# Two score tiles lengthened by 32 bytes, so that the tiles behind them start at multiples of 128 bytes

## The chip, the cores and the metric

The kernel runs on one core of one Trainium2 chip. The metric is device microseconds of one execution; a comparison is made between medians of several executions on the same chip. Before the change the median of three runs is 1702.7 us (1699.94 to 1705.26).

## What is computed

Two layers of a diffusion trunk over 256 latent tokens (x) and 256 context tokens (ctx), width 1024, in 32-bit floats. Cut to what matters:

```python
for i in range(2):
    x   = x   + 0.5 * gt1 * swiglu(modulate(x,   g1, sh1, sc1), ffn1_wi[i], ffn1_wo[i])
    ctx = ctx + 0.5 * cg1 * swiglu(modulate(ctx, g1, ch1, cs1), ffn1_wi[i], ffn1_wo[i])
    hx, hc = modulate(x, g2, sh2, sc2), modulate(ctx, g2, ch2, cs2)
    if i == 0:   # convolution module, width 31, latent and context apart
        y_lat, y_ctx = conformer_conv(hx, ...), conformer_conv(hc, ...)
    else:        # 16 query heads, 4 key heads, window 128, sink, all context keys
        y_lat, y_ctx = windowed_gqa_sink(hx, hc, ...)
    x = x + gt2 * y_lat
    x = x + 0.5 * gt3 * swiglu(modulate(x, g3, sh3, sc3), ffn2_wi[i], ffn2_wo[i])
    if i == 0:   # the context is dropped after layer 1's mixer
        ctx = ctx + cg2 * y_ctx
        ctx = ctx + 0.5 * cg3 * swiglu(modulate(ctx, ...), ffn2_wi[i], ffn2_wo[i])
return rmsnorm(x, final_g)

def swiglu(h, w_in, w_out):          # w_in 1024 x 5632, w_out 2816 x 1024
    gate, up = jnp.split(h @ w_in, 2, axis=-1)
    return (silu(gate) * up) @ w_out
```

## The kernel before, in words

**Products.** Each 32-bit number is split into a high part (hi, rounded to the matmul's fp32r format) and the rest (lo). A product is three matmuls: hi weights with high values, hi weights with low values, lo weights with high values (`mm3`, lines 222, 223 and 224). The helper is `mm3(o, wh, wl, xh, xl, first, last)`: the weights are the stationary operand (128x128, loaded before each matmul), the values are the moving operand that is streamed through, with 512 columns where latent and context tokens go together and 256 where one of them goes alone.

**Tiles.** Normalised values lie in HH (high) and HL (low), eight slices of 512 columns, 2048 bytes of a partition each. The middle values of an FFN lie in MH and ML in the same way; the same memory holds QH and QL of attention. Blocks of weights (1 MB) come by DMA into `raw`, ScalarE writes `hi`, VectorE or GpSimd writes `lo`, four buffers of each. The FFN (`ffn`) takes a block for each of 22 slices of the middle (`g` and `u` accumulate the gate and the up product, `glu_end` writes `sg`, `mt` and then MH and ML) and 12 blocks for the way out (`o`). Layer 1's first FFN and its last have the same code; the last runs on the latent tokens alone (256 columns).

**Where other operands are streamed.** In attention, `qkv_mm` makes the values the stationary operand for k in (4, 5): there a `hi` or `lo` weight tile is the moving one (`o<-hi,HH`). In the convolution `taps_t` streams slices of UH and UL: for channel group 4 one contiguous piece of 256 columns per tap, whose start goes 4 bytes further with every tap (`uh[:, k:k + T]`): tap 16 starts 16 bytes over a multiple of 128, tap 17 starts 20 over, tap 28 starts 64 over. The normalisation streams `dg` (line 280).

**Memory.** The program places tiles once, pool behind pool in the order in which they are opened (const, rawp, hip, lop, adap, work, small, hp, mp). A pool holds, for each tag, its number of buffers times the longest tile that is ever asked of the tag. So one longer tile in a tag moves everything behind it, in the whole program. `mt` is a tag of the pool work with two buffers: in the FFNs a tile of 512 numbers (2048 bytes), in attention a score tile of 528 (2112 bytes), of which 513 are used (`homes`, line 1074).

The addresses that the built program gives, in bytes of a partition, and what is left over a multiple of 128:

| tile | before | over | after | over |
|---|---|---|---|---|
| hi (4), lo (4) | 67200 and on, 99968 and on | 0 | the same | 0 |
| mt (2) | 145216, 147328 | 64, 0 | 145216, 147360 | 64, 32 |
| sg (2) | 149440, 151488 | 64 | 149504, 151552 | 0 |
| t2, sq (2 each) | 153536 and on | 64 | 153600 and on | 0 |
| dg (2) | 157760, 158784 | 64 | 157824, 158848 | 0 |
| HH | 160448 | 64 | 160512 | 0 |
| HL | 176832 | 64 | 176896 | 0 |
| MH, QH | 193216 | 64 | 193280 | 0 |
| ML, QL | 209600 | 64 | 209664 | 0 |

Slices of HH, HL, MH and ML begin 1024 or 2048 bytes apart, so what is left over a multiple of 128 is that of the tile.

**Order.** In the FFNs a scheduler orders the work of each engine; in the start, the convolution and attention it is written out by hand (the strings SEQ, SEQ2 and SEQ3). Neither reads an address.

Of the kernel before, what the change touches and what calls it, by code (L numbers as in the profile page):

```python
# [11 lines left out]
F32 = mybir.dt.float32  # L12
# [5 lines left out]
P = 128  # L18
# [74 lines left out]
def trunk(ctx, tc, a, out):  # L93
# [6 lines left out]
    work = ctx.enter_context(tc.tile_pool(name="work", bufs=2))  # L100
# [969 lines left out]
    homes = []  # L1070
    for _ in range(3):
        z = adap.tile([P, 2, 520], F32, tag="adaw", name="S")
        homes.append([z[:, h, :513] for h in range(2)])
    homes.append([work.tile([P, 528], F32, tag="mt", name="S")[:, :513] for _ in range(2)])
    soft, PT, acc_wo = {}, {}, {}

    def scores(i):
# [232 lines left out]
def _build(nc, arrays):  # L1310
    aps = {k: nc.dram_tensor(f"in_{k}", v.shape, mybir.dt.from_np(v.dtype), kind="ExternalInput").ap()
           for k, v in arrays.items()}
    out = nc.dram_tensor("out_0", (P, CT, T), F32, kind="ExternalOutput").ap()
    with tile.TileContext(nc, schedule_with_timeline_sim=True) as tc:
        trunk(tc, aps, out)
# [12 lines left out]
```

## Time and profile before

| | |
|---|---|
| median of 3 runs | 1702.7 us (1699.94 to 1705.26) |
| profiled execution, its own time | 1699.08 us |
| its span, first to last instruction | 1697.3 us |
| mean granted TensorE clock | 0.98 |
| TensorE matmul busy | 97% of the span |
| VectorE, GpSimd, ScalarE busy | 66%, 48%, 36% |
| DMA | 252.14 MB, mean 149 GB/s |

A busy time of TensorE is the union of its matmuls, which overlap: a matmul's own duration is longer than the distance from its start to the next one's start. Where matmuls follow each other without a wait, that distance, the pitch, is what one more matmul costs. It is read from the timeline as the difference of two starts over the number of matmuls between them.

### The profile page before, as it was taken

Reading aid. Unit: us, or ns where it says so; the run is one execution under the profiler, and the core shown is the slowest. Engines: PE = TensorE matmul, PEld = TensorE weight load, DVE = VectorE, ACT = ScalarE, POOL = GpSimd, SP = SyncE. Lnnn points to the kernel's source line nnn. Section 1 sums busy time; section 2 is a strip of 40 time slices with the busy share of each in tenths; the row PEclk is TensorE's granted clock in tenths of the full one; section 3 lists DMA queues with packets and bytes.
Section 4 is the critical chain, followed back from the end, with each engine's and each line's share of the span. In section 5 each row is a group of like instructions: output and inputs, shape, how many; then the busy total and the mean of one; then the engine's idle time right before and its main releaser. Section 6 shows DMA issues by size and latency. Waiting matters only on the chain.

```text
span 1697.3 us, 23550 instructions
## 1 busy us (share of the span) xinstructions
PE 1644.3 (97%) x9333; PEld 1421.3 (84%) x9333; DVE 1114.0 (66%) x1717; ACT 612.4 (36%) x1015; POOL 811.0 (48%) x614
## 2 busy tenths in 40 slices
PE   9999999998898899999999999999999999999997
PEld 7788888888788888888888898888888888889997
DVE  4597789757799785745546376776545376567553
ACT  3522222234445663212222333222222245555443
POOL 2234324254867654556565546585565437410013
PEclk8999999999999899999999999999999989989999
DMA  7655455441213333433443324455554212246452
GB/s 280 235 181 198 167 186 213 159 149 52 98 63 136 137 114 111 186 138 117 150 154 138 111 75 149 175 193 203 175 196 155 100 50 76 90 169 237 164 193 69
DMA packets 48638, 252.14 MB, mean 149 GB/s; under 512 B 5264, under 2 KB 7312, under 8 KB 30992
## 3 DMA queue, kind: packets, MB, share of 16 engines
q1 hardware_dynamic: 48528, 250.64, 41.2%
q8 instruction: 73, 1.20, 0.3%
q14 instruction: 37, 0.30, 0.1%
HBM read 249.57 MB, written 1.05 MB: 148 GB/s over the span
## 4 chain that ended last, share of the span: by engine, by line
PE 85%; DVE 8%; issue 3%; ACT 2%; POOL 1%; DMA 1%; POOLq 0%; DVEq 0%; SPq 0%; ACTq 0%
PE o L222 9%; PE o L223 9%; PE o L224 9%; PE g L222 8%; PE u L222 8%; PE g L224 8%; PE g L223 8%; PE u L224 8%; PE u L223 8%; DVE A L725 3%; PE gu L544 2%; PE ug L222 1%; DVE HL L337 1%; PE ug L223 1%; PE ug L224 1%
## 5 line engine op out<-in xcount | busy, mean ns | idle before, releaser
L186 POOL TENSOR_TENSOR lo<-raw,hi 128x512 fp32r<-128x512 f32 (+1 forms) x388 | 602.9, 1585 | 683.3 <-ACT hi L183 543.6
L183 ACT ACTIVATE hi<-raw 128x1024 fp32r<-128x1024 f32 (+3 forms) x344 | 278.4, 866 | 575.6 <-PE u L223 256.2
L244 DVE CUSTOM_DVE_ANT_0 junk<-adaw,srow,par 128x1024 bf16<-128x1024 f32 x224 | 384.6, 1717 | 5.4 <-DMA adaw<-in_adaT 0.7
L222 PE MATMUL o<-MH,hi 128*128 128x512 f32 (+1 forms) x788 | 269.6, 344 | 0.0
L224 PE MATMUL o<-MH,lo 128*128 128x512 f32 (+1 forms) x788 | 268.1, 342 | 0.0
L223 PE MATMUL o<-ML,hi 128*128 128x512 f32 (+1 forms) x788 | 268.0, 342 | 0.0
L223 PE MATMUL g<-HL,hi 128*128 128x512 f32 (+1 forms) x712 | 251.8, 355 | 5.3 <-DVE HL L337 5.3
L222 PE MATMUL g<-HH,hi 128*128 128x512 f32 (+1 forms) x712 | 252.9, 357 | 2.8 <-ACT HH L333 2.8
L222 PE MATMUL u<-HH,hi 128*128 128x512 f32 (+1 forms) x712 | 252.9, 356 | 0.0
L224 PE MATMUL u<-HH,lo 128*128 128x512 f32 (+1 forms) x712 | 252.2, 354 | 0.0
L224 PE MATMUL g<-HH,lo 128*128 128x512 f32 (+1 forms) x712 | 252.2, 354 | 0.0
L223 PE MATMUL u<-HL,hi 128*128 128x512 f32 (+1 forms) x712 | 251.5, 353 | 0.0
L228 DVE TENSOR_TENSOR ML<-mt,MH 128x512 fp32r<-128x512 f32 (+1 forms) x92 | 106.2, 1154 | 129.0 <-ACT MH L227 128.9
L224 PEld LDWEIGHTS o<-MH,lo 128*128 128x128 f32 x788 | 147.8, 188 | 19.1
L223 PEld LDWEIGHTS o<-ML,hi 128*128 128x128 f32 x788 | 147.8, 188 | 18.2
L222 PEld LDWEIGHTS o<-MH,hi 128*128 128x128 f32 x788 | 147.6, 188 | 18.0 <-ACT MH L227 0.3
L354 DVE SCALAR_TENSOR_TENSOR X<-o,g,X 128x256 f32<-128x256 f32 x168 | 75.2, 479 | 126.5 <-PE o L224 126.4
L406 DVE TENSOR_TENSOR mt<-sg,u 128x512 f32<-128x512 f32 (+1 forms) x89 | 53.0, 595 | 159.4 <-PE u L224 141.7
L223 PEld LDWEIGHTS g<-HL,hi 128*128 128x128 f32 x712 | 134.0, 189 | 25.7 <-DVE HL L337 6.4
L222 PEld LDWEIGHTS g<-HH,hi 128*128 128x128 f32 x712 | 134.2, 189 | 22.5 <-ACT HH L333 3.9
L224 PEld LDWEIGHTS g<-HH,lo 128*128 128x128 f32 x712 | 134.4, 189 | 20.2
L224 PEld LDWEIGHTS u<-HH,lo 128*128 128x128 f32 x712 | 134.3, 189 | 20.3
(205 smaller groups left out, 2565.2 us busy)
## 6 DMA issues: line engine op xcount, KB each, us to landing
raw<-in_wi SPq DMA_DIRECT2D x85, 1024.0 KB, 4.9
adaw<-in_adaT SPq DMA_DIRECT2D x128, 512.0 KB, 3.7
raw<-in_wo SPq DMA_DIRECT2D x32, 896.0 KB, 4.8
raw<-in_wo SPq DMA_DIRECT2D x20, 1024.0 KB, 5.6
raw<-in_pw SPq DMA_DIRECT2D x12, 1024.0 KB, 4.8
raw<-in_dwd SPq DMA_DIRECT2D x8, 1024.0 KB, 4.9
ch<-in_ada SPq DMA_DIRECT2D x6, 1024.0 KB, 11.0
raw<-in_qkv SPq DMA_DIRECT2D x6, 1024.0 KB, 4.8
```

The costliest lines, as they stand in the source:

```text
L183: nc.scalar.activation(out=hi[:, q:q + w], in_=raw[:, q:q + w], func=AF.Copy)
L186: eng.tensor_tensor(out=lo[:, z:e], in0=raw[:, z:e], in1=hf[:, z:e], op=ALU.subtract)
L222: nc.tensor.matmul(o, wh, xh, start=first, stop=False)
L223: nc.tensor.matmul(o, wh, xl, start=False, stop=False)
L224: return nc.tensor.matmul(o, wl, xh, start=False, stop=last)
L228: return i_, nc.vector.tensor_tensor(out=lo, in0=src, in1=hif, op=ALU.subtract)
L244: nc.vector.tensor_tensor_reduce(out=junk, in0=wt, in1=srow[:, s, :], scale=1.0, scalar=pcol(O_ADAB, 72 * l + t), op0=ALU.mult, op1=ALU.ad ...
L337: return nc.vector.scalar_tensor_tensor(out=HL[:, c, SL[s]], in0=t2, scalar=sh, in1=HHf[:, c, SL[s]], op0=ALU.add, op1=ALU.subtract)
L354: return nc.vector.scalar_tensor_tensor(out=X[:, c, SL[s]], in0=psrc, scalar=gate, in1=X[:, c, SL[s]], op0=ALU.mult, op1=ALU.add)
L406: nc.vector.tensor_tensor(out=mt[:, :n], in0=sg[:, :n], in1=u[:, :n], op=ALU.mult)
L544: nc.tensor.matmul(gu[k][q], w[:, o:o + P], h[:, c, :], start=c == 0 and h is HH and w is hi, stop=c == 7 and w is lo)
L725: nc.vector.scalar_tensor_tensor(out=d, in0=src(k, z), scalar=wk(c, k), in1=d, op0=ALU.mult, op1=ALU.add)
```

## The change

The two score tiles of the tag `mt` get 536 numbers where they had 528, so each of the two buffers of the tag is 32 bytes longer. What is used of them stays 513 numbers. All that lies behind the first of the two moves: the second buffer by 32 bytes, everything behind it by 64. Each engine has the same instructions in the same order as before, and the DMA queues the same transfers.

```diff
@@ -1071,7 +1071,7 @@
     for _ in range(3):
         z = adap.tile([P, 2, 520], F32, tag="adaw", name="S")
         homes.append([z[:, h, :513] for h in range(2)])
-    homes.append([work.tile([P, 528], F32, tag="mt", name="S")[:, :513] for _ in range(2)])
+    homes.append([work.tile([P, 536], F32, tag="mt", name="S")[:, :513] for _ in range(2)])
     soft, PT, acc_wo = {}, {}, {}
```

## Rows read from the trace of the kernel before

**Rows 1.** The page: busy time of TensorE, and the chain that ended last by engine.
```profile
PE 1644.3 (97%) x9333; PEld 1421.3 (84%) x9333; DVE 1114.0 (66%) x1717; ACT 612.4 (36%) x1015; POOL 811.0 (48%) x614
...
PE 85%; DVE 8%; issue 3%; ACT 2%; POOL 1%; DMA 1%; POOLq 0%; DVEq 0%; SPq 0%; ACTq 0%
```

**Rows 2.** Busy time by stretch (an FFN; 1.5 us of attention): columns as its header says.
```profile
core 0: us, PE busy (x) PEld busy (x) DVE busy (x) ACT busy (x) POOL busy (x), PEclk, DMA share, GB/s
170.00:400.00 230.00, 230.00 (x1086) 192.16 (x1085) 171.89 (x230) 61.56 (x85) 83.61 (x53) 1.00 0.45 165
1373.00:1374.50 1.50, 1.50 (x9) 1.50 (x9) 1.09 (x3) 0.76 (x2) 0.00 (x0) 0.50 0.90 382
```

**Rows 3.** Timeline (start us, us, engine line op): TensorE at 1373, granted clock 0.50.
```profile
1373.20 0.41 PE L223 MATMUL o<-HL,hi 128*128 128x256 f32 x1
...
1374.27 0.41 PE L222 MATMUL o<-HH,hi 128*128 128x256 f32 x1
```

**Rows 4.** Timeline: TensorE in layer 0's first FFN, first and last of 28 matmuls.
```profile
199.79 0.39 PE L224 MATMUL u<-HH,lo 128*128 128x512 f32 x1
...
205.97 0.39 PE L224 MATMUL g<-HH,lo 128*128 128x512 f32 x1
```

**Rows 5.** Timeline: TensorE in the last FFN, first and last of 19 matmuls.
```profile
1599.77 0.28 PE L223 MATMUL u<-HL,hi 128*128 128x256 f32 x1
...
1601.89 0.28 PE L223 MATMUL g<-HL,hi 128*128 128x256 f32 x1
```

**Rows 6.** Groups by line and shape: matmuls whose moving operand is HH, HL, MH or ML.
```profile
L222 PE MATMUL u<-HH,hi 128*128 128x512 f32 x472 | 185.5, 393 | 0.0
...
L222 PE MATMUL o<-MH,hi 128*128 128x512 f32 x444 | 174.3, 393 | 0.0
...
L223 PE MATMUL o<-ML,hi 128*128 128x256 f32 x344 | 96.0, 280 | 0.0
...
L223 PE MATMUL o<-HL,hi 128*128 128x256 f32 x288 | 82.5, 290 | 2.8 <-DVE HL L337 2.7
...
L224 PE MATMUL u<-HH,lo 128*128 128x256 f32 x240 | 67.6, 282 | 0.0
...
L223 PE MATMUL ug<-HL,hi 128*128 128x512 f32 x96 | 38.2, 398 | 0.0
```

**Rows 7.** Timeline: weight tiles as moving operand in attention, first and last of 25 matmuls.
```profile
1399.27 0.28 PE L224 MATMUL o<-hi,HL 128*128 128x256 f32 x1
...
1401.99 0.28 PE L224 MATMUL o<-hi,HL 128*128 128x256 f32 x1
```

**Rows 8.** Timeline: the same kind 10 us later, first and last of 14 matmuls.
```profile
1411.35 0.28 PE L223 MATMUL o<-lo,HH 128*128 128x256 f32 x1
...
1412.88 0.28 PE L224 MATMUL o<-hi,HL 128*128 128x256 f32 x1
```

**Rows 9.** Timeline: HH and HL as moving operand at 634, five matmuls in a row.
```profile
634.04 0.28 PE L224 MATMUL g<-HH,lo 128*128 128x256 f32 x1
...
634.49 0.28 PE L223 MATMUL g<-HL,hi 128*128 128x256 f32 x1
```

**Rows 10.** Timeline: first matmul of taps 16, 17, 18, 28 and 29 (three matmuls each).
```profile
564.69 0.28 PE L222 MATMUL o<-UH,hi 128*128 128x256 f32 x1
...
565.02 0.28 PE L222 MATMUL o<-UH,hi 128*128 128x256 f32 x1
...
565.39 0.29 PE L222 MATMUL o<-UH,hi 128*128 128x256 f32 x1
...
568.98 0.28 PE L222 MATMUL o<-UH,hi 128*128 128x256 f32 x1
...
569.33 0.28 PE L222 MATMUL o<-UH,hi 128*128 128x256 f32 x1
```

**Rows 11.** Timeline: VectorE, two products into the tag mt, one for each buffer.
```profile
203.42 0.68 DVE L406 TENSOR_TENSOR mt<-sg,u 128x512 f32<-128x512 f32 x1
...
215.93 0.68 DVE L406 TENSOR_TENSOR mt<-sg,u 128x512 f32<-128x512 f32 x1
```

## The prediction

> **What bounds the kernel now.** I read the page first, then the stretches, then the timeline matmul by matmul, since the change moves no instruction and can only alter what one of them takes.
>
> The page [rows 1] shows TensorE with matmuls in flight for 97% of the span; the chain that ended last runs through TensorE for 85% of it, with VectorE second at 8%. A stretch inside an FFN [rows 2] shows the same sharper: 230.00 of 230.00 us busy, the next engine, VectorE, at 171.89 (75%). So what decides there is how fast one matmul follows another. I call that distance from start to start the pitch.
>
> [...] The trace has more: (205.97 - 199.79) / 27 = 228.9 ns for 512 columns [rows 4] and (1601.89 - 1599.77) / 18 = 117.8 ns for 256 [rows 5]. [...]
>
> **What the change can touch.** It moves HH, HL, MH, ML and dg from 64 bytes over a multiple of 128 to a multiple. Counting the FFN and projection matmuls that stream them [rows 6]: with 512 columns, 472 in each of six groups (g and u, three lines), 444 in each of three (o), 96 in each of three (ug): 2832 + 1332 + 288 = 4452. With 256 columns, 344 in three, 288 in three, 240 in six: 1032 + 864 + 1440 = 3336. Two smaller groups are left out. Together 7788. Weight tiles do not move.
>
> **Is a pitch at a multiple of 128 different?** The trace holds such matmuls. In attention some take a weight tile, which lies at a multiple of 128, as the streamed operand: (1401.99 - 1399.27) / 24 = 113.3 ns [rows 7] against the 117.8 of [rows 5]. That is 4.5 ns less for the same 256 columns, the same clock, the same three-part product. The taps of the convolution add a scale of starts [rows 10]: tap 16, 16 bytes over a multiple of 128, has (565.02 - 564.69) / 3 = 110 ns (to 3 ns, the rounding of two starts); tap 17, 20 over, (565.39 - 565.02) / 3 = 123; tap 28, 64 over, (569.33 - 568.98) / 3 = 117. So a streamed operand's start does alter the pitch, in steps of about 4.5 to 6 ns, and 64 over is on the middle step, even where the tile lies in another part of memory than HH.
>
> But two rows speak against a plain rule. The same weight tiles, still at a multiple of 128, run at (1412.88 - 1411.35) / 13 = 117.7 ns a few microseconds later [rows 8], and HH itself, 64 over, runs once at (634.49 - 634.04) / 4 = 112.5 ns [rows 9]. Either level can be had at either start; how a run of matmuls begins has a part in it. What differs is how often: of the six unbroken runs with weight tiles streamed, five settle on the lower level; of some sixty with HH or MH, three. I read this as: the multiple of 128 makes the lower step likely, not certain.
>
> [...]
>
> **The sum.** The 256-column matmuls: one step, 4.5 ns, from [rows 5, 7]: 3336 x 4.5 = 15.0 us. For 512 columns the trace has no row at a multiple of 128, so the price is bounded. Upper end: if the loss goes with the columns, it is twice the step, 9.0 ns, 4452 x 9.0 = 40.1 us; that fits the pitches, since 228.9 - 9.0 and 117.8 - 4.5 both leave about 6.6 ns over the bare columns. Lower end: nothing, since the 256-column rows say nothing of a stream during which the next weights have long been loaded. I take one step here too, 4.5 ns, the row it is nearest to and the only step that a row of one shape shows [rows 5, 7]: 4452 x 4.5 = 20.0 us. A loss at 512 is the third rival below.
>
> Not all of it reaches the end. The chain is on TensorE for 85% of the span while it is busy for 97% [rows 1]; the rest of its work lies beside VectorE and others in the convolution and between attention's steps. I count 85 / 97 = 0.88: (15.0 + 20.0) x 0.88 = 30.8 us. In the FFN stretch a pitch 2% shorter lifts VectorE from 75% to 76% of the time and DMA from 0.45 to 0.46 [rows 2], so no other engine becomes late there.
>
> The rest costs nothing that I can find. VectorE's products into the two mt buffers take 0.68 us each, though one lies 64 over and the other at 0 [rows 11]; so 32 over or the moved sg, t2 and sq should not matter, and if they did, VectorE's idle quarter in an FFN would take it (if not covered, 1% on its 171.89 us is 1.7 us in such a stretch). Score tiles hold the same 513 numbers. DMA goes to tiles that do not move, but for six column chunks in the start.
>
> The profiled execution took 1699.08 us, 3.6 below the median of 1702.7; 1699.1 - 30.8 = 1668.3 for such an execution, **1672 us** for the median.
>
> **The rivals.**
> *No change.* The lower level depends on how a run begins [rows 8, 9], or on the stationary operand: in [rows 7] that was HH, 64 over, and it is weights at a multiple of 128 in the FFNs before and after. Then the long runs stay on the step they have now and the time is 1702.7. For it: the 512-column pitch is one and the same in the FFN stretch, so I see no second level there at all. Against it: taps 16 and 28 [rows 10] have weights at a multiple of 128 in both cases and still differ. [...]
> *More: the loss goes with the columns.* 512 columns gain 9.0 ns: (15.0 + 40.1) x 0.88 = 48.5 us, 1654. The other way, 256 columns alone: 13.2 us, 1689.5. Both are ends of my forecast.
> *Slower.* Streamed tile and weights then both start at multiples of 128, and TensorE reads both at the same time (weight loads fill 192.16 of the 230 us [rows 2]). If reads that start alike get in each other's way, the pitch goes one step up instead of down, to the 123 of tap 17 [rows 10], 5.5 ns above 117.8: 7788 x 5.5 x 0.88 = 37.7 us, 1740. It decides as soon as the pitch of [rows 4] rises at all, for no engine could give it back. Against it: taps have weights at multiples of 128, and tap 16, nearly so itself, is the fastest of them.
> *The change does not do what it says* is ruled out: the built program's addresses are as in the table.
>
> **How the numbers follow.** About 0.3% (5 us) is what a measurement of this kernel can tell from no change; the runs shown differ by that. Forecast, a lower pitch with an end between 1654 and 1690: 0.57, of which a third for each of its three prices (both shapes one step, 512 two steps, 256 alone). No change: 0.34, since two rows contradict the plain rule. Slower by the collision: 0.09. All of the forecast's cases lie more than 5 us below 1702.7. The likeliest case's own range is 1650 to 1692. The range that should hold 8 in 10 must take in no change with its spread, up to 1707, and below the larger price without the factor 0.88: 1702.7 - 55.1 = 1647.6, so 1647. The slower case is left out.
>
> **What would show it.** In the profile after: a run of 512-column matmuls in the first FFN with a pitch of 224.4 ns (220 at the one end, 228.9 at the other); a run of 256 columns in the last FFN at 113.3; a TensorE busy time lower by about 30 us with the same count of instructions; VectorE and GpSimd busy as before. I am wrong if both pitches stand where they are, or if they fall and the span does not: then the time has turned into waits of TensorE, on VectorE's ML or HL or on weights, which the groups' idle times would name.

## The result, and the profile after

The changed kernel is slower: 1721.2 us (1719.15 to 1722.07, 4 runs) against 1702.28 (1699.94 to 1705.26), a ratio of 1.0108 [1.0092, 1.0124], or 18.9 us. The forecast was 1672 with a range up to 1707: the direction was wrong.

The page of the changed kernel, busy time by engine and the chain that ended last by engine, answers to [rows 1]:

```profile
PE 1668.0 (97%) x9333; PEld 1431.6 (83%) x9333; DVE 1114.7 (65%) x1717; ACT 612.2 (36%) x1015; POOL 809.5 (47%) x614
...
PE 85%; DVE 8%; issue 3%; ACT 2%; POOL 1%; DMA 1%; POOLq 0%; SPq 0%; DVEq 0%; ACTq 0%
```

TensorE has the same 9333 matmuls and is busy 23.7 us longer. VectorE, ScalarE and GpSimd stay within 1.5 us of what they were, and the chain has the same shares: no new wait, only slower matmuls.

TensorE's order is the same in both, so the two traces can be laid beside each other matmul by matmul. Between number 1000 and number 1750, a stretch of 512 columns without a wait, the kernel before has these two (timeline; start us, duration us, engine, line, operation):

```profile
206.20 0.39 PE L222 MATMUL g<-HH,hi 128*128 128x512 f32 x1
...
377.87 0.39 PE L222 MATMUL o<-MH,hi 128*128 128x512 f32 x1
```

and the changed kernel the same two, and below them numbers 8250 and 9250, a stretch of 256 columns in the last FFN:

```profile
212.54 0.39 PE L222 MATMUL g<-HH,hi 128*128 128x512 f32 x1
...
386.82 0.39 PE L222 MATMUL o<-MH,hi 128*128 128x512 f32 x1
...
1581.69 0.28 PE L223 MATMUL o<-ML,hi 128*128 128x256 f32 x1
...
1700.36 0.28 PE L224 MATMUL o<-MH,lo 128*128 128x256 f32 x1
```

The pitch of 512 columns was (377.87 - 206.20) / 750 = 228.9 ns, as in [rows 4], and is (386.82 - 212.54) / 750 = 232.4. For 256 columns it was 117.8 [rows 5] and is (1700.36 - 1581.69) / 1000 = 118.7. With the prediction's counts that is 4452 x 3.5 + 3336 x 0.9 = 15.6 + 3.0 = 18.6 us of the 18.9 measured. The two profiled executions differ by more, 1722.07 - 1699.08 = 23.0 us. Of this 4.3 lie ahead of matmul 250, which starts at 43.52 us before and at 47.81 after; in the kernels below it starts anywhere from 43.4 to 46.9, without regard to their distances, so this part is most likely scatter of the start.

The same change shows where the prediction took its evidence from. Weight tiles as streamed operand, which ran at 113.3 ns in [rows 7], in the changed kernel, first and last of 29 matmuls in a row:

```profile
1419.76 0.28 PE L223 MATMUL o<-lo,HH 128*128 128x256 f32 x1
...
1423.08 0.28 PE L224 MATMUL o<-hi,HL 128*128 128x256 f32 x1
```

(1423.08 - 1419.76) / 28 = 118.6 ns. The streamed tile hi has not moved; only HH and HL have, which are the weights there. So the low pitch did not belong to the streamed tile's own start.

### The profile page after: what moved, and what is told of

Same layout as the page of the kernel before. It is cut to its first block, busy times and chain, and to the rows that moved or that the text cites. A ratio compares the mean times of both kernels' runs of the same rounds, so it can differ in the third digit from the quotient of the medians.

```text
span 1720.3 us, 23550 instructions
## 1 busy us (share of the span) xinstructions
PE 1668.0 (97%) x9333; PEld 1431.6 (83%) x9333; DVE 1114.7 (65%) x1717; ACT 612.2 (36%) x1015; POOL 809.5 (47%) x614
## 4 chain that ended last, share of the span: by engine, by line
PE 85%; DVE 8%; issue 3%; ACT 2%; POOL 1%; DMA 1%; POOLq 0%; SPq 0%; DVEq 0%; ACTq 0%
PE o L222 9%; PE o L223 9%; PE o L224 9%; PE g L223 8%; PE g L222 8%; PE g L224 8%; PE u L222 8%; PE u L223 8%; PE u L224 8%; DVE A L725 3%; PE gu L544 2%; PE ug L222 1%; PE ug L223 1%; DVE HL L337 1%; PE ug L224 1%
## 5 line engine op out<-in xcount | busy, mean ns | idle before, releaser
L222 PEld LDWEIGHTS u<-HH,hi 128*128 128x128 f32 x712 | 134.7, 189 | 20.9
L223 PEld LDWEIGHTS u<-HL,hi 128*128 128x128 f32 x712 | 134.7, 189 | 20.8
```

Of the source, the lines that this page charges most:

```text
L222: nc.tensor.matmul(o, wh, xh, start=first, stop=False)
L223: nc.tensor.matmul(o, wh, xl, start=False, stop=False)
```

## The experiments

The rows leave two theories. A: the pitch depends on the **distance** between the start of the streamed tile and that of the weights, modulo some power of two. B: it depends on the streamed tile's own start. By the table of addresses, hi and lo lie 128 bytes over a multiple of 256; HH, HL, MH and ML lay 192 over before and lie 0 over after. The distance, streamed less weights modulo 256, was 64 and is 128. The expectations of the first runs still count it modulo 128, where the change has distance 0; that the period is 256 came out of the scan.

### Both moved together, from the kernel before and from the changed one

```diff
     b1 = const.tile([P, CT], F32, name="b1")
+    const.tile([P, 16], F32, name="pad")
```

64 bytes at the end of the first pool move weights and streamed tiles alike. In the first run the streamed tiles then lie at multiples of 128, as the change has them, at the old distance; in the second, made from the changed kernel, they lie 64 over, as before, at the new distance.

> The kernel before, with 64 bytes put ahead of the streamed blocks, so that weights (hi, lo) lie 64 over a multiple of 128 and HH, HL, MH, ML at a multiple: the streamed tiles are where the change has them, and their distance to the weights is that of before. Theory A (the distance between streamed tile and weights, modulo 128, sets the pitch): as before, 512 columns at 228.9 ns, about 1702 us. Theory B (the streamed tile's own start sets it, a multiple of 128 being the worse): as after, 232.3 ns on average, about 1721 us. Theory C (neither; another moved tile, such as mt or sg, makes VectorE or ScalarE late): pitch 228.9 and some time between.

> The changed kernel with the same 64 bytes: streamed tiles and weights both lie 64 over a multiple of 128. Theory A (distance, here 0): 232.3 ns, about 1721 us. Theory B (own start, here 64): 228.9 ns, about 1702 us.

Measured: 1700.35 us, ratio 0.999 [0.9977, 1.0003], and 1723.3, ratio 1.0128 [1.0112, 1.0145]. Numbers 1000 and 1750 in the timeline of the first:

```profile
207.60 0.39 PE L222 MATMUL g<-HH,hi 128*128 128x512 f32 x1
...
379.27 0.39 PE L222 MATMUL o<-MH,hi 128*128 128x512 f32 x1
```

and of the second:

```profile
211.60 0.39 PE L222 MATMUL g<-HH,hi 128*128 128x512 f32 x1
...
385.89 0.39 PE L222 MATMUL o<-MH,hi 128*128 128x512 f32 x1
```

171.67 / 750 = 228.9 and 174.29 / 750 = 232.4 ns. Streamed tiles at multiples of 128 cost nothing at the old distance, and tiles back at 64 over gain nothing at the new one. Theory B falls, and with it the reason of the forecast.

### The middle values alone

```diff
     X = const.tile([P, CT, 2 * T], F32, name="X")
+    mp.tile([P, 16], F32, name="pad")
     HH = hp.tile([P, CT, 2 * T], F32R, name="HH")
```

Only MH and ML move, from distance 64 to 128.

> The kernel before, with 64 bytes put ahead of MH and ML alone: those two lie at multiples of 128, HH, HL, dg, sg, t2 and mt stay. Theories A and B: the matmuls o<-MH go to 232.3 (512 columns) and 118.8 ns (256), those that stream HH stay at 228.9 and 117.8; the time rises by 1332 x 3.4 + 1032 x 1.0 ns = 5.6 us, to about 1708 us. Theory C: all pitches and the time as before.

Measured: 1706.63 us, ratio 1.003 [1.0018, 1.0042]. Timeline, first and last of 168 matmuls in a row with MH or ML, then of 336 with HH or HL (the lines are one higher here):

```profile
246.38 0.39 PE L223 MATMUL o<-MH,hi 128*128 128x512 f32 x1
...
285.18 0.40 PE L225 MATMUL o<-MH,lo 128*128 128x512 f32 x1
285.41 0.40 PE L223 MATMUL g<-HH,hi 128*128 128x512 f32 x1
...
362.10 0.39 PE L225 MATMUL u<-HH,lo 128*128 128x512 f32 x1
```

(285.18 - 246.38) / 167 = 232.3 ns for the moved tiles, (362.10 - 285.41) / 335 = 228.9 for the others, in the same FFN with the same weights. In the last FFN the two kinds run at 118.6 and 117.8. The 1332 and 1032 matmuls with MH or ML [rows 6] times 3.5 and 0.8 ns make 5.5 us; 4.6 were measured.

### Matmuls alone, by distance

The kernel is cut down to its products: 48 matmuls for each case, three-part as in mm3, with weights w bytes and streamed tile m bytes over a multiple of 256.

```diff
+            for r in range(reps):
+                kt, q = r % 4, r % 8
+                wh = W[:, w // 4 + q * P:w // 4 + q * P + P]
...
+                xh = M[:, m // 4 + kt * 512:m // 4 + kt * 512 + n]
...
+                for t, (u, v) in enumerate(((wh, xh), (wh, xl), (wl, xh))):
+                    nc.tensor.matmul(o[:, :n], u, v, start=r == 0 and t == 0, stop=r == reps - 1 and t == 2)
```

> Only matmuls, one run of 48 per case (hi weights with two values, lo weights with one, as in the kernel), weights 0, 32, 64 or 96 over a multiple of 128, streamed tile 0 to 240 over in steps of 16, and 4, 8, 12, 20; nothing else of the layers is computed. Theory A: weights 0 with streamed 0 gives 232.3 ns for 512 columns, streamed 64 gives 228.9, weights 64 with streamed 64 gives 232.3, and the pitch is a function of the difference. Theory B: the pitch is a function of the streamed start alone, whatever the weights' start. If neither holds, all aligned starts have one pitch here.

It took 506.9 us. Its timeline puts a case into one row (n columns, w, m in the output's name); the start of the next row less its own start, over 48, is the pitch, to some 0.5 ns, since the step from one case to the next is in it.

```profile
29.65 11.04 PE L129 MATMUL n512w0m0x<-M,W 128*128 128x512 f32 x48
40.53 11.28 PE L129 MATMUL n512w0m16x<-M,W 128*128 128x512 f32 x48
...
74.05 11.16 PE L129 MATMUL n512w0m64x<-M,W 128*128 128x512 f32 x48
85.05 11.25 PE L129 MATMUL n512w0m80x<-M,W 128*128 128x512 f32 x48
...
118.44 11.32 PE L129 MATMUL n512w0m128x<-M,W 128*128 128x512 f32 x48
129.59 11.36 PE L129 MATMUL n512w0m144x<-M,W 128*128 128x512 f32 x48
...
163.23 11.35 PE L129 MATMUL n512w0m192x<-M,W 128*128 128x512 f32 x48
174.42 11.42 PE L129 MATMUL n512w0m208x<-M,W 128*128 128x512 f32 x48
...
196.88 11.05 PE L129 MATMUL n512w0m240x<-M,W 128*128 128x512 f32 x48
207.77 5.91 PE L129 MATMUL n256w0m0x<-M,W 128*128 128x256 f32 x48
213.51 5.87 PE L129 MATMUL n256w0m16x<-M,W 128*128 128x256 f32 x48
...
275.84 5.62 PE L129 MATMUL n256w0m192x<-M,W 128*128 128x256 f32 x48
281.30 5.88 PE L129 MATMUL n256w0m208x<-M,W 128*128 128x256 f32 x48
...
365.00 11.07 PE L129 MATMUL n512w64m64x<-M,W 128*128 128x512 f32 x48
375.91 11.37 PE L129 MATMUL n512w64m96x<-M,W 128*128 128x512 f32 x48
```

| distance modulo 256 | 0 | 16 | 64 | 112 | 128 | 192 | 208 | 240 |
|---|---|---|---|---|---|---|---|---|
| 512 columns, ns | 226.7 | 231.7 | 229.2 | 231.0 | 232.3 | 233.1 | 234.6 | 226.9 |
| 256 columns, ns | 119.6 | 119.0 | 117.7 | 113.3 | 118.5 | 113.8 | 119.2 | 117.3 |

Without any other work the two pitches of the kernels come back at 64 and 128, to 0.3 ns. Weights and streamed tile both 64 over have (375.91 - 365.00) / 48 = 227.3 ns, that of distance 0; weights 64 over and streamed tile 0 over, distance 192, have 233.3. So it is the distance, and a distance of -64 is one of 192. All twelve cases of 512 columns with the weights moved by 32, 64 or 96 bytes lie within 0.9 ns of the case with the same distance modulo 256. The recorded expectation of theory A had the period wrong: at 128 bytes, distance 0 would have had the 232.3 ns of distance 128, and it has 226.7. The two shapes have their best distances in different places. The eight steps of 16 that are left out lie between 230.8 and 234.4 ns for 512 columns.

### Fewer weight columns, and finer steps

```diff
-                wh = W[:, w // 4 + q * P:w // 4 + q * P + P]
+                wh = W[:, w // 4 + q * P:w // 4 + q * P + cols]
...
```

> Only matmuls, runs of 48 a case as in the first scan, weights at a fixed place, nothing else of the layers computed. Theory A, now with the first scan's period of 256 bytes: distances 0, 64 and 128 repeat 226.7, 228.8 and 232.5 ns for 512 columns; distance 112 repeats 113.3 ns for 256 columns, and each case has the same pitch wherever it stands in the sequence. If the loss comes from weights being read while values stream, cases with 64 or 32 weight columns instead of 128 (half and a quarter of the weight read) lose less at every distance: 512 columns well under 226. Rival D (the loss is the streamed read's own, crossing boundaries of memory): the pitch at each distance is the same with 128, 64 and 32 weight columns. Steps of 4 bytes around the best distances: starts that are no multiple of 16 are 2 to 6 ns slower.

It took 338.77 us. Rows as above, c the number of weight columns:

```profile
29.21 11.08 PE L129 MATMUL n512c128m0x1y<-M,W 128*128 128x512 f32 x48
40.13 11.17 PE L129 MATMUL n512c128m64x0y<-M,W 128*128 128x512 f32 x48
51.13 11.32 PE L129 MATMUL n512c128m128x1y<-M,W 128*128 128x512 f32 x48
62.29 11.21 PE L129 MATMUL n512c64m0x0y<-M,W 128*64 128x512 f32 x48
...
95.30 11.27 PE L129 MATMUL n512c32m0x1y<-M,W 128*32 128x512 f32 x48
106.41 11.29 PE L129 MATMUL n512c32m64x0y<-M,W 128*32 128x512 f32 x48
117.53 11.23 PE L129 MATMUL n512c32m128x1y<-M,W 128*32 128x512 f32 x48
128.61 11.36 PE L129 MATMUL n512c128m224x0y<-M,W 128*128 128x512 f32 x48
...
173.37 11.51 PE L129 MATMUL n512c128m240x0y<-M,W 128*128 128x512 f32 x48
184.72 11.68 PE L129 MATMUL n512c128m244x1y<-M,W 128*128 128x512 f32 x48
```

With all 128 weight columns distances 0, 64 and 128 have 227.5, 229.2 and 232.5 ns, as in the first scan. With 64 they have 230.0, 228.5 and 229.2, with 32 they have 231.5, 231.7 and 230.8: hardly any dependence is left, but the mean of the three distances is hardly lower with 64 (229.2 ns against 229.7) and higher with 32 (231.3). So with less weight read the stream as a whole was no faster. All distances seem to share a part beyond the columns: 256 columns at a granted clock of 0.50 went at (1374.27 - 1373.20) / 5 = 214 ns [rows 3], and if that were columns alone, twice the columns at twice the clock would take 214 ns too. By this estimate even the 226.7 ns of distance 0 hold some 13 ns more, for which no run shows a cause. And distance 240 has (184.72 - 173.37) / 48 = 236.5 ns here, against 226.9 in the first scan: a distance can have more than one level, that is, more than one pitch on which a run of matmuls settles.

The finer steps start at no multiple of 16 bytes. At 256 columns they have 117.7 to 123.1 ns, against 114.0 to 114.4 for distances 112 and 192 in this scan, as expected. At 512 columns, from 228 to 252, they have 229.0 to 239.8: all slower than the 226.9 of the first scan, but some are faster than the 236.5 that distance 240 has here.

### The kernel at distances 0 and 240

```diff
-    homes.append([work.tile([P, 528], F32, tag="mt", name="S")[:, :513] for _ in range(2)])
+    homes.append([work.tile([P, 520], F32, tag="mt", name="S")[:, :513] for _ in range(2)])
```

The score tiles are shortened by the 32 bytes that the change adds: the streamed tiles again lie at multiples of 128, but at distance 0.

> The score tiles of the tag mt 520 numbers long instead of 528: HH, HL, MH, ML lie at multiples of 128, as in the change, but 0 instead of 128 from the weights modulo 256. Theory A with period 256: 512 columns 226.7 ns (2.2 less than before), 256 columns 120.0 (2.2 more): 4452 x -2.2 + 3336 x 2.2 ns = -2.5 us, about 1699 us, and in the trace the two shapes have moved in opposite directions. Theory B (own start at a multiple of 128 is the bad one): 232.3 and 118.8, 1721 us.

Measured: 1701.09 us, ratio 0.9993 [0.9981, 1.0006]. Numbers 1000, 1750, 8250 and 9250 in its timeline:

```profile
206.78 0.39 PE L222 MATMUL g<-HH,hi 128*128 128x512 f32 x1
...
376.78 0.39 PE L222 MATMUL o<-MH,hi 128*128 128x512 f32 x1
...
1559.40 0.28 PE L223 MATMUL o<-ML,hi 128*128 128x256 f32 x1
...
1679.40 0.28 PE L224 MATMUL o<-MH,lo 128*128 128x256 f32 x1
```

170.00 / 750 = 226.7 and 120.00 / 1000 = 120.0 ns: 4452 x 2.2 = 9.8 us gained and 3336 x 2.2 = 7.3 lost. Both terms came as forecast, and nearly cancel.

For distance 240, HH, HL, MH and ML are used from 16 bytes into longer tiles behind a pad:

```diff
+    hp.tile([P, 40], F32, name="pad")
+    wide = CT * 2 * T + 64
...
+    OFF = 4
+    HHt = hp.tile([P, wide], F32R, name="HH")
...
+    HH, HL = at(HHt, OFF), at(HLt, OFF)
```

> The kernel before with HH, HL, MH and ML lengthened by 64 numbers each and used from 16 bytes in, so that they lie 240 bytes from the weights modulo 256. Theory A: 512 columns 226.7 ns, 256 columns 117.1: 4452 x -2.2 + 3336 x -0.7 ns = -12 us, about 1690 us. Theory B: the start is 112 over a multiple of 128, and theory B has no price for it but no reason for a gain: 1702 us.

Measured: 1732.96 us, ratio 1.0189 [1.0168, 1.021], a clear miss. Numbers 1000 and 1750:

```profile
213.61 0.40 PE L230 MATMUL g<-HH,hi 128*128 128x512 f32 x1
...
391.11 0.40 PE L230 MATMUL o<-MH,hi 128*128 128x512 f32 x1
```

177.50 / 750 = 236.7 ns, on the upper level that distance 240 had in the second scan. Even that is not all: behind a wait at 501 us the same kernel's 512 columns run at 233.3 ns (336 matmuls in a row take 78.40 us), and from 1043 us on, after a stretch of 256 columns, at 236.7 again, so this distance has shown three levels. The 256 columns came as forecast, 117.1 ns.

### Distance 192, and a distance for each shape

```diff
-    homes.append([work.tile([P, 528], F32, tag="mt", name="S")[:, :513] for _ in range(2)])
+    homes.append([work.tile([P, 544], F32, tag="mt", name="S")[:, :513] for _ in range(2)])
```

The tiles are lengthened by twice as much as in the change: the streamed tiles lie 64 over a multiple of 128, as before.

> The score tiles of the tag mt 544 numbers long: HH, HL, MH, ML lie 64 over a multiple of 128, as before, but 192 instead of 64 from the weights modulo 256. Theory A with period 256: 512 columns 233.4 ns (4.5 more than before), 256 columns 113.3 (4.5 less): 4452 x 4.5 - 3336 x 4.5 ns = +5 us, about 1707 us, the two shapes apart in opposite directions. A rule with period 128, of the distance or of the own start: 228.9 and 117.8 as before, 1702 us.

Measured: 1711.28 us, ratio 1.0067 [1.0049, 1.0085]. Numbers 1000, 1750, 8250 and 9250:

```profile
210.57 0.40 PE L222 MATMUL g<-HH,hi 128*128 128x512 f32 x1
...
385.57 0.40 PE L222 MATMUL o<-MH,hi 128*128 128x512 f32 x1
...
1577.90 0.28 PE L223 MATMUL o<-ML,hi 128*128 128x256 f32 x1
...
1691.24 0.28 PE L224 MATMUL o<-MH,lo 128*128 128x256 f32 x1
```

175.00 / 750 = 233.3 ns, 4.4 above the kernel before: 19.6 us lost. 113.34 / 1000 = 113.3, 4.5 below: up to 15.0 us gained. The net loss against the runs beside it is 10.2, so the 256 columns gave back some 9 of those 15; in other stretches, such as 118 matmuls in a row from 388 us on, they run at 117.8 ns.

The lower level is not reserved to distance 192. In the first run above, at the old distance of 64, the same 118 matmuls, with nothing between them, have these two as first and last:

```profile
382.02 0.28 PE L222 MATMUL o<-MH,hi 128*128 128x256 f32 x1
...
395.28 0.28 PE L222 MATMUL o<-MH,hi 128*128 128x256 f32 x1
```

(395.28 - 382.02) / 117 = 113.3 ns, where the kernel before, at the same distance, has 117.8. At 256 columns distances 64 and 192 thus share two levels; 192 is mostly on the lower, 64 almost always on the upper.

The last kernel puts these together: distance 0 while there are 512 columns, and from the normalisation that layer 1's first FFN does in its middle on (`mid`), 192 bytes further into the same tiles. The score tiles are those of the run at distance 0, and HH, HL, MH and ML lie in longer tiles as in the run at distance 240; the switch is

```diff
-    ffn(1, 0, (0, 1), pre_ctx=lambda: norm(1, 1, 0), mid=lambda: norm(0, 1, 1), per_block=lambda: ada(2))
+    def narrow():
+        nonlocal off, HH, HL, HHf
+        off = 48
+        HH, HL, HHf = at(HHt, off), at(HLt, off), at(HHt, off).bitcast(F32)
+        norm(0, 1, 1)
+
+    ffn(1, 0, (0, 1), pre_ctx=lambda: norm(1, 1, 0), mid=narrow, per_block=lambda: ada(2))
```

> Distance 0 (score tiles of 520 numbers) while the streamed operand has 512 columns, and from attention on, where it has 256, HH and HL, and in the last FFN MH and ML, are used from 192 bytes further in. Theory A: 512 columns 226.7 ns, 256 columns 113.3 in attention and in the last FFN and 120.0 before; 4452 x -2.2 + 2064 x -4.5 + 1272 x 2.2 ns = -16 us, about 1686 us, if TensorE bounds throughout. Rival E (an FFN on 256 columns is bound by the weights that arrive, not by the pitch): the last FFN is as long as before, about 1697 us.

Measured: 1691.01 us (1684.22 to 1700.32, 12 runs), ratio 0.9947 [0.9926, 0.9968]: faster than both kernels. Timeline of its last FFN, numbers 7800 and 8100, then 8250 and 9250:

```profile
1501.43 0.28 PE L229 MATMUL g<-HL,hi 128*128 128x256 f32 x1
...
1535.43 0.28 PE L229 MATMUL u<-HL,hi 128*128 128x256 f32 x1
...
1553.29 0.28 PE L229 MATMUL o<-ML,hi 128*128 128x256 f32 x1
...
1671.07 0.28 PE L230 MATMUL o<-MH,lo 128*128 128x256 f32 x1
```

34.00 / 300 = 113.3 ns, and 117.78 / 1000 = 117.8. Rival E falls for the first stretch: 300 matmuls there took 36.00 us in the run at distance 0, so the arriving weights do not bind. Between the two, at 1540 us, TensorE waits once; behind that wait it is on the upper level and keeps it to the end of the FFN. These some 1180 matmuls cost 1180 x 4.5 = 5.3 us, about what the median lacks to the 1686 that was expected. Eight of its runs lie at 1684 to 1692 us, with a mean granted clock of 0.980 to 0.982, and four at 1697 to 1700, at 0.976 to 0.978: so the clock very likely has a part in what parts them, and whether the level has one too is not shown, since only one of them has a trace.

## Why the prediction was wrong

**What bounds the kernel** held: TensorE runs through long parts of the FFNs without a wait, and there what the pitch rises by arrives in the time (numbers 1000 to 1750: 171.67 us before, 174.28 after).

**The counts and addresses** held: 4452 and 3336 matmuls account for 18.6 of 18.9 us.

**The step that failed** is "a streamed operand's start does alter the pitch": I read 113.3 against 117.8 ns [rows 5, 7] as a tile at a multiple of 128 against one 64 over. No run shows such a step of a tile's own start: moved along with the weights, from 64 over to a multiple, the streamed tiles keep 228.9 and 117.8 ns. In [rows 7] both operands differ from [rows 5]: the weight tile is streamed and HH is the stationary one. The distance there is 128 - 192 = -64, that is 192, and 113.3 ns is what distance 192 can give (256 columns in the scan, and the kernel at distance 192). The change takes this distance to 128 as well, and the same instructions then run at 118.6; in the kernels at distances 0 and 192, where HH as weights gives distances 0 and 64, they settle at 120.0 and 117.8, with the weight tiles always in the same place. And the 4.5 ns are not even the price of a distance: they are what lies between the two levels that distances 64 and 192 share, while at 128, where the change leads, only 118.7 and, in a few stretches, 120.0 were seen in long unbroken runs of HH and MH. In the sum, the two terms of 15.0 and 20.0 us gained became 3.0 and 15.6 us lost. The rival "no change" had named the stationary operand as a possible cause, and how a run begins as another, and both have a part (232.4 and 228.9 ns for the same streamed start modulo 256, in the changed kernel and in the first run; 113.3 and 117.8 ns before and behind the wait in the last one); I weighed the operand by the taps [rows 10], where three matmuls in a row are all there is of a start, and the start changes every three. The scan has no 110 ns at distance 16, so the taps gave no settled pitch.

**The rows that spoke against it** were not noise. [rows 8] at 117.7 ns with the same tiles is the second level of distance 192, which two of the experiments show as well. [rows 9], five matmuls at 112.5 ns at distance 64, is that of distance 64: the 118 matmuls at 113.3 ns in the first run repeat it. The prediction said that either level can be had at either start, and that holds; what it took from there, that a multiple of 128 makes the lower one likely, does not. What decides the level stays open.

**Carrying one step over to 512 columns** failed apart from that: the two shapes do not share a scale. Distance 0 is the best for 512 columns (226.7) and about the worst for 256 (120.0); at 192 it is nearly the other way round (233.3 and 113.3). The 6.6 ns over the bare columns, by which the prediction found its 9.0 ns fitting, rest on a time of the columns alone at full clock that no run shows; the lowest pitches that the runs showed are 226.7 ns for 512 columns and, for 256, 113.3 in runs of 25 matmuls and more.

**The factor 0.88** was too small: a sum of 18.6 us without it gives the 18.9 measured. These matmuls are mostly in FFN stretches where nothing else holds TensorE up, between numbers 1000 and 1750 for one, and there all of it arrives; the share of the whole span does not apply to them.

**The rival "slower"** had the right kind of cause, the relation of the two streams, and its test, that the pitch of [rows 4] need only rise, held. Its price was too high, 5.5 ns for both shapes against 3.5 and 0.9, and its reason was wrong: both operands at the same place modulo 256 is not the collision but the best case for 512 columns (226.7 ns). The change leads to distance 128, so that the sign came out right is luck.

## What to carry to other kernels

Where TensorE streams fp32r matmuls without a wait, as here, look at where streamed tile and weights lie to each other: in these kernels, with the same matmuls throughout, it took the median from 1691.01 to 1732.96 us. Any tile that is lengthened ahead of one of the two can move it: after each change of a pool, look at the pitch of an unbroken run before looking for a wait. Choose the distance for the shape that does most of the work, by a small scan, and run the kernel at it, since a distance with several levels can land on the wrong one (240: 226.9 ns in the scan, 236.7 in the kernel), and change it behind a wait (there to 233.3). A row that differs from another in two operands proves nothing about one of them.

## What the runs showed of the hardware

- In these runs the pitch of the fp32r matmuls, with a weight load each, goes with the distance of the two starts modulo 256 bytes: in the scan 226.7 to 234.6 ns for 512 columns in steps of 16 bytes, 113.3 to 120 for 256. Why 256, and why the shapes differ, no run tells.
- With 32 weight columns the dependence is nearly gone at the three distances tried (230.8 to 231.7 ns, against 227.5 to 232.5 with 128), and the mean pitch no lower (231.3 ns against 229.7).
- Some distances have several levels (240: 226.9, 233.3 and 236.5 to 236.7 ns at 512 columns; 64 and 192: 113.3 and 117.8 at 256). A run of matmuls can keep its level for hundreds of matmuls (1000 at 117.8 ns in the last kernel), and behind a single wait it can be another, as at 1540 us in the last kernel (113.3, then 117.8 ns) and at 501 us in the one at distance 240 (236.7, then 233.3). What sets the level is open.
